# Hybrid decoder layer: a second buffer for the convolution phases, early gate results on ScalarE's queue, the last merged block by halves, first and last stage regrouped

## The chip, the cores and the metric

The kernel runs on one core of one Trainium2 chip. A core has TensorE (PE in the profile), VectorE (DVE), ScalarE (ACT), GpSimd (POOL) and SyncE (SP), which work side by side, each through its own instructions in order, and wait for each other by semaphores. Transfers between DRAM and the on-chip memory are issued by SP, POOL or ACT and carried by 16 DMA engines. The metric is the time of one execution on the device in microseconds (us), as a median over several runs.

## The reference

One layer of a decoder on 1024 tokens of 1024 channels, all in float32. A gated mixer runs a causal depthwise convolution of 31 taps and an attention of 8 heads on the same projected input, merges the two through sigmoid gates, and a SwiGLU block follows.

```python
def hybrid_mixer(h, ...):
    proj = h @ w_in
    glu_in, qkv, gates = jnp.split(proj, [2 * CONV_WIDTH, 2 * CONV_WIDTH + 3 * ATT_WIDTH], axis=-1)
    u_val, u_gate = jnp.split(glu_in, 2, axis=-1)
    u = u_val * jax.nn.sigmoid(u_gate)
    u = causal_depthwise_conv(u, conv_w, conv_b)
    u = jax.nn.silu(layernorm(u, conv_ln_g, conv_ln_b))
    y_conv = u @ w_conv_out
    o = stick_breaking_attention(q, k, v)
    y_att = o.reshape(b, s, ATT_WIDTH) @ w_att_out
    g_conv, g_att = jnp.split(gates, 2, axis=-1)
    merged = jax.nn.sigmoid(g_conv) * y_conv + jax.nn.sigmoid(g_att) * y_att
    return merged @ w_o

def reference(x, c, ...):
    h = rmsnorm(x, pre_mix_g[l]) * (1.0 + sc1) + sh1
    y = hybrid_mixer(h, ...)
    x = x + ga1 * rmsnorm(y, post_mix_g[l])
    h = rmsnorm(x, pre_ffn_g[l]) * (1.0 + sc2) + sh2
    gate, up = jnp.split(h @ w_ffn_in, 2, axis=-1)
    y = (silu(gate) * up) @ w_ffn_out
    return x + ga2 * rmsnorm(y, post_ffn_g[l])
```

## The kernel before, in words

Activations lie with the channels on the 128 partitions and the tokens along the row. A large product keeps float32 accuracy by splitting each operand into a rounded high part (copied by ScalarE) and a low part (the difference, taken by VectorE): each product of two tiles is then three TensorE matmuls, high by high, high by low and low by high. The gate products and the SwiGLU block save one product in eight by a Strassen-like scheme, whose sums and differences VectorE forms. A scheduler places the instructions of each engine before the kernel runs, from the order of the code, priorities and the buffers' free times; once placed, an engine's order is fixed.

The stages that the change touches, in order of time:

- **First stage.** `rstd`, shifts and scales, then for each of the eight channel blocks k the products of three weight blocks (`pq0`, `pk0`, `pgg0`) by `gemm_k`. ScalarE and VectorE are pinned to the order of the code, TensorE isn't.
- **Convolution.** `conv(ct)` runs for four blocks of 128 channels (ct 0 to 3), with the attention heads between. The gated input `u` is stored to `v_d[ct]` and read back transposed into `ph` (L440 to L442), whose first columns POOL sets to zero. Then 40 tile products per block, 20 for each half, go through TensorE (`pcv`, L453; each is two records in the trace) with five weight tiles `cvw`, which rotate through three buffers. Both the stores (`v_d`, `u_d`) and the loads (`ph`, `cvw`) stand in SP's queue, in order. `ph` has one buffer, so the load of `ph` for one block is issued when the products of the block before have read it.
- **Early gate products.** For seven gate pairs i, `early(i, q)` forms two of the seven products of the scheme with q 0 and 1 in one PSUM bank `k` out of three. After each, ScalarE reads the bank into `ee` (L624), one of two buffers `sg` of 256 KB, and the result goes to DRAM (`e_d0`, shown as `e_d`, or `s_d`) by `store`, which is POOL's queue (L101). The next user of a bank waits for its `ee`, and an `ee` waits until the store of the one two before has landed. At the same time SP loads sixteen pieces of the input (`f<-xm_d`, 256 KB each), from which VectorE forms operands (L674 to L677) that ScalarE and VectorE split into `T1o` to `T4o` (L147, L660).
- **Merge.** For each of eight blocks n: two products `pya`, VectorE multiplies by the gate (L840) and adds (L841), and `split_r` splits the 1024 columns of the block into `mhi` (ScalarE) and `mlo` (VectorE). The output product `pwo` (L900) then takes, in its first pass, the first 512 columns of each block.
- **Last stage.** The second product of the SwiGLU block (`ka`, L1524) in sweeps, the norm and the residual. `x_tile` has four buffers, `acc` two and `rs` two.

The profile's line numbers are those of the kernel before. After the change lines from L370 on are 3 higher, and from the merge on 11 higher.

Of the kernel before, what the change touches and what calls it, by code (L numbers as in the profile page):

```python
# [10 lines left out]
F32 = mybir.dt.float32  # L11
F32R = mybir.dt.float32r
AF = mybir.ActivationFunctionType
ALU = mybir.AluOpType
# [3 lines left out]
P = 128  # L18
D = 1024
T = 1024  # L20
KT = D // P
CH = 512
# [47 lines left out]
def tile_block(ctx: ExitStack, tc: tile.TileContext, xT, vecs, ada1, ada2, win, wv, wcv, wat, wo, w1, w2, cvw, out):  # L70
# [29 lines left out]
    def store(dst, src):  # L100
        nc.gpsimd.dma_start(dst, src)  # L101
# [97 lines left out]
    with ExitStack() as s0:  # L199
# [146 lines left out]
        for k in range(KT):  # L346
# [18 lines left out]
            if k <= 1:  # L365
                for i in range(k + 1):
                    gemm_k(ws[i], w0s[i], k)
                for kk in range(k + 1):
                    gemm_k(ws[k + 1], w0s[k + 1], kk)
            else:  # L370
                for b_, w_ in zip(ws, w0s):
                    gemm_k(b_, w_, k)
        high.__exit__(None, None, None)
        pin(begin, START_PIN)
# [32 lines left out]
    with ExitStack() as sC:  # L407
        pc = mkpool(sC, "pc")
        with ExitStack() as sA:
# [28 lines left out]
            def conv(ct):  # L438
                ph = pc.tile([P, NG, SH - 1 + TM], F32, tag="ph", name=f"ph{ct}", bufs=1)
                pool.memset(ph[:, :, 0:SH - 1], 0.0)  # L440
# [174 lines left out]
            def early(i, q):  # L615
# [8 lines left out]
                act.activation(e, k, (AF.Copy, AF.Sigmoid)[q])  # L624
                store(s_d[2 * i][:, :CH] if q else e_d0[i], e)

# [7 lines left out]
    with ExitStack() as sG:  # L634
# [195 lines left out]
        for n in range(KT):  # L830
# [6 lines left out]
            for c in range(NCH):  # L837
# [3 lines left out]
                dve.tensor_tensor(y[:, cs], y[:, cs], sg[c], op=ALU.add)  # L841
            hi, lo = split_r(y, (f"mhi{n}", f"mlo{n}"), act, dve)
            mhi.append(hi)
            mlo.append(lo)
        assert not a2
# [643 lines left out]
    with ExitStack() as sG:  # L1489
# [10 lines left out]
        def x_tile(name):  # L1500
            return px.tile([P, 2, CH], F32, tag="xr", name=name, bufs=4)

# [134 lines left out]
        def sum_sq(name, ys):  # L1637
            acc = pg.tile([P, CH], F32, tag="acc", name=name, bufs=2)
            for n, y in enumerate(ys):
                if n == 0:  # L1640
                    act.activation(acc, y, AF.Square)
                else:
                    sq = sq_tile(f"{name}_{n}")
                    act.activation(sq, y, AF.Square)
                    add(dve, acc, acc, sq)
            return acc

        def finish(c, h, ps_sum, yy, last=None):
            n = ps_sum.shape[-1]
            cols = slice(h * n, (h + 1) * n)  # L1650
            dcols = slice(c * CH + h * n, c * CH + (h + 1) * n)
            rs = pg.tile([P, CH], F32, tag="rs", name=f"frs{c}{h}", bufs=2)[:, :n]
            m, a = (sq_tile(f"frs{c}{h}{i}")[:, :n] for i in "ma")
# [162 lines left out]
```

## Time and profile before

| | us |
|---|---|
| median of 3 runs | 1413.03 (1412.89 to 1413.87) |
| the profiled execution's own time | 1414.92 |
| its span, first to last instruction | 1413.2 |
| ScalarE busy | 655.3 (46%) |
| VectorE busy | 1048.3 (74%) |
| GpSimd busy | 117.4 (8%) |

The mean clock granted to TensorE is 0.990 of full speed. A row of the timeline reads: start in us, duration in us, engine, line, operation, output tile <- input tiles, shapes, how many such instructions stand behind one another (x), and in brackets how long the engine sat idle before it and what ended that. A row of waits reads: engine and line that waited <- what released it, us in total, times, longest. Consecutive matmuls overlap, so the distance of their starts, not their duration, is what one costs.

### The profile page before, as it was taken

What the parts mean: (1) busy time and instruction counts of PE and PEld (TensorE: products, weight loads), DVE (VectorE), ACT (ScalarE), POOL (GpSimd) and SP (SyncE); (2) the same over time, 40 slices, a digit from 0 to 9 for tenths busy, and PEclk for the clock granted to TensorE, in tenths of its full rate; (3) what the DMA queues carried; (4) which work ended last, traced back from release to release, by engine and by line L of the source; (5) the groups of instructions that cost most, each with busy time, mean ns of one, the idle gap of its engine ahead of it and who ended that gap; (6) DMA issues with size and microseconds to landing.
All of it is one profiled execution on the core that took longest, in us unless ns stands there. A gap on an engine that the chain in (4) does not pass through costs nothing.

```text
span 1413.2 us, 18854 instructions
## 1 busy us (share of the span) xinstructions
PE 1378.3 (98%) x6810; PEld 1157.3 (82%) x6810; DVE 1048.3 (74%) x1591; ACT 655.3 (46%) x1146; POOL 117.4 (8%) x262
## 2 busy tenths in 40 slices
PE   7999999999998999999999999999999999999996
PEld 5898898998886788788877778888888887888886
DVE  7897687675865888878589878778877776785355
ACT  6375566364554455512356553334434443434441
POOL 0100001000001111000011110001111110000002
PEclk8999999999999999999999999999999999999998
DMA  9512051140348554973934545456777769586736
GB/s 382 200 39 82 16 164 30 46 150 30 120 150 298 208 170 148 349 226 124 360 120 163 182 148 177 165 171 212 260 250 246 264 240 387 177 337 221 254 116 120
DMA packets 93789, 265.02 MB, mean 188 GB/s; under 512 B 10048, under 2 KB 21440, under 8 KB 92672
## 3 DMA queue, kind: packets, MB, share of 16 engines
q1 hardware_dynamic: 74352, 201.68, 42.0%
q0 software_dynamic: 19344, 62.14, 12.4%
q8 instruction: 53, 0.87, 0.3%
q14 instruction: 40, 0.33, 0.1%
HBM read 192.74 MB, written 71.04 MB: 187 GB/s over the span
## 4 chain that ended last, share of the span: by engine, by line
PE 75%; issue 9%; DVE 8%; DMA 4%; ACT 2%; POOL 1%; SPq 0%; DVEq 0%; POOLq 0%; ACTq 0%
PE ka L982 14%; PE ka L1524 9%; PE kc L982 8%; PE pwo L900 6%; PE pb L1524 4%; PE pgv L168 3%; PE pv L473 3%; PE pgg L168 2%; PE pk L168 2%; PE pq L168 2%; PE ke L1090 2%; PE pcv L453 2%; PE tr L566 2%; PE pa L1524 2%; PE kb L982 2%
## 5 line engine op out<-in xcount | busy, mean ns | idle before, releaser
L545 ACT ACTIVATE ka<-z 128x128 f32<-128x128 f32 (+2 forms) x96 | 47.0, 496 | 55.8 <-PE z L544 51.9
L551 DVE TENSOR_TENSOR_SCAN ka<-ka,eye 128x128 f32<-128x128 f32 (+1 forms) x64 | 52.1, 831 | 23.2 <-ACT ka L545 23.0
L570 DVE TENSOR_TENSOR alo<-tr,ahi 128x512 fp32r<-128x512 f32 x80 | 53.4, 685 | 21.3 <-ACT ahi L569 20.7
L569 ACT ACTIVATE ahi<-tr 128x512 fp32r<-128x512 f32 x80 | 46.7, 603 | 39.1 <-PE av L575 22.9
L1524 PE MATMUL ka<-gt,w2f 128*128 128x512 f32 x264 | 63.4, 389 | 0.0
L556 DVE TENSOR_TENSOR be<-be,ka 128x127 f32<-128x127 f32 (+2 forms) x96 | 51.2, 550 | 12.1 <-ACT be L547 8.5
L1524 PEld LDWEIGHTS ka<-gt,w2f 128*128 128x128 f32 x264 | 49.5, 188 | 10.3
L123 DVE SCALAR_TENSOR_TENSOR ada<-ada,cb 128x1024 f32<-128x1024 f32 x32 | 38.9, 1223 | 23.6 <-DMA ada<-in_ada_dram 23.4
L1090 PE MATMUL ke<-b,w_hi 128*128 128x512 f32 x176 | 55.2, 395 | 0.0
L547 ACT ACTIVATE be<-z 128x127 f32<-128x127 f32 (+2 forms) x96 | 46.4, 496 | 17.8 <-PE tr L566 17.6
L566 PE MATMUL tr<-ident,be 128*128 128x128 f32 x288 | 46.6, 272 | 0.0
L453 PE MATMUL pcv<-ph,cvw 128*128 128x128 f32 x320 | 43.7, 282 | 2.5 <-DMA ph<-v_d 2.5
L554 DVE TENSOR_TENSOR_SCAN ka<-ka 128x512 f32<-128x512 f32 x32 | 40.4, 1274 | 6.3 <-ACT ka L545 6.3
L404 PE MATMUL k<-hhi,a 128*128 128x512 f32 x112 | 38.3, 413 | 6.6 <-ACT ee L624 6.6
L453 PEld LDWEIGHTS pcv<-ph,cvw 128*128 128x128 f32 x320 | 41.5, 198 | 3.5 <-issue 2.7
L575 PE MATMUL av<-ahi,vst 128*128 128x256 f32 x160 | 43.8, 291 | 0.0
L576 PE MATMUL av<-alo,vst 128*128 128x256 f32 x160 | 42.2, 290 | 0.0
L1090 PEld LDWEIGHTS ke<-b,w_hi 128*128 128x128 f32 x176 | 32.9, 188 | 7.9 <-issue 1.0
L147 ACT ACTIVATE gt<-X 128x512 fp32r<-128x512 f32 x33 | 20.3, 629 | 39.4 <-DVE X L1567 14.3
L473 PE MATMUL pv<-wv_hi,hhi 128*128 128x256 f32 x128 | 36.7, 287 | 1.6 <-DVE vst L478 0.9
L147 ACT ACTIVATE s1o<-s 128x512 fp32r<-128x512 f32 x22 | 13.8, 629 | 48.8 <-PE ka L982 41.0
L473 PE MATMUL pv<-wv_lo,hhi 128*128 128x256 f32 x128 | 36.3, 285 | 0.0
(545 smaller groups left out, 4145.8 us busy)
## 6 DMA issues: line engine op xcount, KB each, us to landing
w_d<-w2o POOLq DMA_DIRECT2D x44, 512.0 KB, 7.6
w2f<-w_d SPq DMA_DIRECT2D x44, 512.0 KB, 4.5
ada<-in_ada_dram SPq DMA_DIRECT2D x32, 512.0 KB, 5.7
w2r<-in_w_dram SPq DMA_DIRECT2D x44, 256.0 KB, 3.8
w1g<-in_w_dram SPq DMA_DIRECT2D x21, 512.0 KB, 3.7
w1u<-in_w_dram SPq DMA_DIRECT2D x21, 512.0 KB, 5.7
cvw<-in_cvw_dram SPq DMA_DIRECT2D x20, 512.0 KB, 3.8
ada_w<-in_ada_dram SPq DMA_DIRECT2D x8, 1024.0 KB, 13.9
```

The costliest lines, as they stand in the source:

```text
L168: pe.matmul(bank, st[:, cols], mv[k][:, c * CH:(c + 1) * CH], start=(i == 0 and s == 0), stop=(i == n - 1 and s == 2))
L453: pe.matmul(cv[:, gi * TM:(gi + 1) * TM], wts[n][:, at:at + P], ph[:, g, SH - 1 - d:SH - 1 - d + TM], start=(d == 0), stop=(d == SH - 1))
L473: pe.matmul(pv[:, :256], st[k][:, tcols], mv[:, wc], start=(k == 0 and i == 0), stop=(k == KT - 1 and i == 2))
L545: act.activation(kap[:, s_lo:s_hi], z[:, zo:zo + w], AF.Sigmoid, bias=0.0, scale=-0.125)
L551: dve.tensor_tensor_scan(rev, rev, eye[:, CH - w:][:, ::-1], 0.0, op0=ALU.mult, op1=ALU.add)
L556: dve.tensor_tensor(beta[:, :m], beta[:, :m], kap[:, s_lo + 1:s_lo + 1 + m], op=ALU.mult)
L566: pe.transpose(tr[:, o:o + P], src, ident)
L570: dve.tensor_tensor(alo, tr, ahi, op=ALU.subtract)
L900: pe.matmul(bank_, st[:, cols], mv[k][:, cs], start=(k == 0 and q == 0), stop=(k == KT - 1 and q == 2))
L982: pe.matmul(bank_, st[:, cols], t[:, mv], start=(first and j == 0 and s == 0), stop=(j == HK - 1 and s == 2), skip_group_check=not first)
L1090: pe.matmul(kbs[f], wes[f][st][:, cols], t[:, mv], start=(i == 0 and j == 0 and q == 0), stop=(j == HK - 1 and q == 2), skip_group_check=i ...
L1524: pe.matmul(dst, w[st][:, cols], g[mv], start=first and s == 0, stop=last and s == 2, skip_group_check=more)
```

## The change

The last two channel blocks of the first stage are taken per weight block. `ph` gets a second buffer. The store of `ee` is issued by ScalarE itself, behind the `ee` that it stores. The last merged block is split in two halves of 512 columns, each with its own `mhi` and `mlo` instruction. In the last stage `x_tile` gets a fifth buffer, `rs` a third, and `acc` and `rs` lie in another pool.

```diff
--- before.py
+++ after.py
@@ -367,9 +367,12 @@
                     gemm_k(ws[i], w0s[i], k)
                 for kk in range(k + 1):
                     gemm_k(ws[k + 1], w0s[k + 1], kk)
-            else:
+            elif k < KT - 2:
                 for b_, w_ in zip(ws, w0s):
                     gemm_k(b_, w_, k)
+        for b_, w_ in zip(ws, w0s):
+            for k in (KT - 2, KT - 1):
+                gemm_k(b_, w_, k)
         high.__exit__(None, None, None)
         pin(begin, START_PIN)
         sg0 = []
@@ -436,7 +439,7 @@
                 load(channels(v_d[ct]), u)
 
             def conv(ct):
-                ph = pc.tile([P, NG, SH - 1 + TM], F32, tag="ph", name=f"ph{ct}", bufs=1)
+                ph = pc.tile([P, NG, SH - 1 + TM], F32, tag="ph", name=f"ph{ct}", bufs=2)
                 pool.memset(ph[:, :, 0:SH - 1], 0.0)
                 load(ph[:, :, SH - 1:], v_d[ct].rearrange("g p m -> p g m"))
                 wts = []
@@ -622,7 +625,7 @@
                 prod0(k, w, ("B11", "B21")[q], q == 0)
                 e = sgp.tile([P, CH], F32, tag="sg", name=f"ee{q}_{i}", bufs=2)
                 act.activation(e, k, (AF.Copy, AF.Sigmoid)[q])
-                store(s_d[2 * i][:, :CH] if q else e_d0[i], e)
+                act.dma_start(s_d[2 * i][:, :CH] if q else e_d0[i], e)
 
             for n, i in enumerate(GPAIRS):
                 early(i, 0)
@@ -839,9 +842,17 @@
                 load(sg[c], s_d[8 + n][:, cs])
                 last = dve.tensor_tensor(sg[c], yb[c], sg[c], op=ALU.mult)
                 dve.tensor_tensor(y[:, cs], y[:, cs], sg[c], op=ALU.add)
-            hi, lo = split_r(y, (f"mhi{n}", f"mlo{n}"), act, dve)
-            mhi.append(hi)
-            mlo.append(lo)
+                if n < KT - 1:
+                    continue
+                if c == 0:
+                    mhi.append(hp.tile([P, T], F32R, tag="act", name=f"mhi{n}"))
+                    mlo.append(hp.tile([P, T], F32R, tag="act", name=f"mlo{n}"))
+                act.activation(mhi[n][:, cs], y[:, cs], AF.Copy)
+                dve.tensor_tensor(mlo[n][:, cs], y[:, cs], mhi[n][:, cs], op=ALU.subtract)
+            if n < KT - 1:
+                hi, lo = split_r(y, (f"mhi{n}", f"mlo{n}"), act, dve)
+                mhi.append(hi)
+                mlo.append(lo)
         assert not a2
         add_bias(16, 32)
         fold_gate(gpost1, 16, C_POST1)
@@ -1498,7 +1509,7 @@
             return hp.tile([P, 2, CH], dt, tag="act", name=name)
 
         def x_tile(name):
-            return px.tile([P, 2, CH], F32, tag="xr", name=name, bufs=4)
+            return px.tile([P, 2, CH], F32, tag="xr", name=name, bufs=5)
 
         def bank(name):
             return psg.tile([P, CH], F32, tag="main", name=name)
@@ -1635,7 +1646,7 @@
             return po_.tile([P, CH], F32, tag="wt", name=name, bufs=3)
 
         def sum_sq(name, ys):
-            acc = pg.tile([P, CH], F32, tag="acc", name=name, bufs=2)
+            acc = px.tile([P, CH], F32, tag="acc", name=name, bufs=2)
             for n, y in enumerate(ys):
                 if n == 0:
                     act.activation(acc, y, AF.Square)
@@ -1649,7 +1660,7 @@
             n = ps_sum.shape[-1]
             cols = slice(h * n, (h + 1) * n)
             dcols = slice(c * CH + h * n, c * CH + (h + 1) * n)
-            rs = pg.tile([P, CH], F32, tag="rs", name=f"frs{c}{h}", bufs=2)[:, :n]
+            rs = px.tile([P, CH], F32, tag="rs", name=f"frs{c}{h}", bufs=3)[:, :n]
             m, a = (sq_tile(f"frs{c}{h}{i}")[:, :n] for i in "ma")
             rstd_from(rs, m, a, ps_sum, D)
             for m in range(4):
```

What it moves in the engines' orders is shown at three places; in the names the numbers at the end tell buffers apart.

TensorE at the change from the convolution of block 2 to that of block 3, before, where `pcv_0_4111` is the first half of block 3, `ph_4108` its input, and `z`, `tr`, `av` belong to the attention (`z_1_5_1` head 1, row block 5):

```order
L576 MATMUL av_0_1_3777<-alo_0_1_0_3817,vst_0_2496 128x256
L543 MATMUL z_1_4_1_3950<-kst_1_3035,qst_1_3033 128x256
L544 MATMUL z_1_4_1_3950<-klo_1_3037,qst_1_3033 128x256
L453 MATMUL pcv_0_4111<-ph_4108,cvw_0_4113 128x128 x8
L453 MATMUL pcv_0_4111<-ph_4108,cvw_1_4123 128x128 x3
L543 MATMUL z_1_5_1_3960<-kst_1_3035,qst_1_3033 128x256
L544 MATMUL z_1_5_1_3960<-klo_1_3037,qst_1_3033 128x256
L453 MATMUL pcv_0_4111<-ph_4108,cvw_1_4123 128x128 x2
```

After, from the first product of block 3 on:

```order
L456 MATMUL pcv_0_4111<-ph_4108,cvw_0_4113 128x128
L546 MATMUL z_1_6_0_3907<-kst_1_3035,qst_1_3033 128x512
L547 MATMUL z_1_6_0_3907<-klo_1_3037,qst_1_3033 128x512
L456 MATMUL pcv_0_4111<-ph_4108,cvw_0_4113 128x128
L546 MATMUL z_1_7_0_3915<-kst_1_3035,qst_1_3033 128x512
L547 MATMUL z_1_7_0_3915<-klo_1_3037,qst_1_3033 128x512
L578 MATMUL av_0_1_3777<-ahi_0_1_1_3803,vst_2_2551 128x256
L579 MATMUL av_0_1_3777<-alo_0_1_1_3804,vst_2_2551 128x256
L578 MATMUL av_0_1_3777<-ahi_0_1_1_3803,vst_2_2551 128x256
L579 MATMUL av_0_1_3777<-alo_0_1_1_3804,vst_2_2551 128x256
L578 MATMUL av_0_1_3777<-ahi_0_1_0_3816,vst_0_2496 128x256
L456 MATMUL pcv_0_4111<-ph_4108,cvw_0_4113 128x128 x4
```

Before, all of the products of block 3 stand behind `z_1_4_1`; after, the first stands ahead of `z_1_6_0` and all that follows it, and when `z_1_5_1` comes, twelve instead of eleven of them have been issued. On SP's queue the load of `ph_4108` now stands two transfers behind the store of its `v_d`, ahead of the last weight tile of block 2 and of all weights of block 3.

ScalarE in the early gate products, before, where `ee_2_4434` is the second result of pair 2 and `T2o_4643` to `T4o_4652` are the operands from the third group of `f`:

```order
L147 ACTIVATE T3o_4625<-f_1_4607 128x512
L624 ACTIVATE ee_3_4416<-k_4400 128x512
L147 ACTIVATE T4o_4628<-f_1_4610 128x512
L147 ACTIVATE a_6_4518<-ew_4515 128x512
L147 ACTIVATE a_6_4554<-ew_4515 128x512
L147 ACTIVATE T2o_4643<-f_2_4633 128x512
L147 ACTIVATE T1o_4646<-f_2_4632 128x512
L147 ACTIVATE T3o_4649<-f_2_4631 128x512
L147 ACTIVATE T4o_4652<-f_2_4634 128x512
L624 ACTIVATE ee_2_4434<-k_4361 128x512
```

After:

```order
L147 ACTIVATE T3o_4625<-f_1_4607 128x512
L147 ACTIVATE a_6_4518<-ew_4515 128x512
L147 ACTIVATE a_6_4554<-ew_4515 128x512
L147 ACTIVATE T4o_4628<-f_1_4610 128x512
L147 ACTIVATE T2o_4643<-f_2_4633 128x512
L147 ACTIVATE T1o_4646<-f_2_4632 128x512
L147 ACTIVATE T3o_4649<-f_2_4631 128x512
L627 ACTIVATE ee_2_4434<-k_4361 128x512
L628 DMA s_d_83<-ee_2_4434 128x512
L147 ACTIVATE T4o_4652<-f_2_4634 128x512
```

`ee_2_4434` moves ahead of `T4o_4652`, `ee_3_4416` (shown before only) ahead of `T2o_4619`, and each `ee` is followed by a transfer that ScalarE issues. On VectorE the operation L676 of the third group, `f_2_4633`, now stands directly behind the low part of `T2o_4619`, where before `f_3_4656` and the low parts of `T1o_4622` and `T3o_4625` came between.

TensorE at the first use of the last merged block (`mhi_6159`, `mlo_6160`) in `pwo_0`, before:

```order
L900 MATMUL pwo_1_6227<-mhi_5913,wo_1_hi 128x512
L900 MATMUL pwo_1_6227<-mlo_5914,wo_1_hi 128x512
L900 MATMUL pwo_1_6227<-mhi_5913,wo_1_lo 128x512
L900 MATMUL pwo_0_6192<-mhi_6159,wo_0_hi 128x512
L900 MATMUL pwo_1_6227<-mhi_5957,wo_1_hi 128x512
L900 MATMUL pwo_1_6227<-mlo_5958,wo_1_hi 128x512
L900 MATMUL pwo_1_6227<-mhi_5957,wo_1_lo 128x512
L900 MATMUL pwo_1_6227<-mhi_5995,wo_1_hi 128x512
```

After (there it is called `mhi_6156`, `mlo_6157`):

```order
L911 MATMUL pwo_1_6229<-mhi_5913,wo_1_lo 128x512
L911 MATMUL pwo_1_6229<-mhi_5957,wo_1_hi 128x512
L911 MATMUL pwo_1_6229<-mlo_5958,wo_1_hi 128x512
L911 MATMUL pwo_0_6194<-mhi_6156,wo_0_hi 128x512
L911 MATMUL pwo_1_6229<-mhi_5957,wo_1_lo 128x512
L911 MATMUL pwo_1_6229<-mhi_5995,wo_1_hi 128x512
L911 MATMUL pwo_1_6229<-mlo_5996,wo_1_hi 128x512
L911 MATMUL pwo_0_6194<-mlo_6157,wo_0_hi 128x512
```

Two more products of `pwo_1` stand ahead of it than before. In the last stage the order of all engines is the same up to the names.

## The prediction

> **What bounds the kernel now.** The first view is the page's list of busy times, the second the list of who waited for whom on TensorE.
>
> ```profile
> span 1413.2 us, 18854 instructions
> PE 1378.3 (98%) x6810; PEld 1157.3 (82%) x6810; DVE 1048.3 (74%) x1591; ACT 655.3 (46%) x1146; POOL 117.4 (8%) x262
> ```
>
> ```profile
> PE k L404 <- ACT ee L624: 6.6, 4, 4.0
> PE pcv L453 <- DMA ph<-v_d: 2.5, 1, 2.5
> PE pwo L900 <- ACT mhi L147: 1.3, 1, 1.3
> PE ka L1524 <- ACT gb L147: 1.2, 1, 1.2
> PE pv L473 <- DVE qst L497: 0.8, 1, 0.8
> ```
>
> TensorE is busy for 1378.3 of 1413.2 us, so only 34.9 us of the span can be won without taking work away from it. The change takes no matmul away and adds none. What it can win is therefore in gaps of TensorE and in the slower clock that follows a gap. Three of the rows above are waits that the change aims at: 6.6 us for the results of the early gate products, 2.5 us for the convolution's input, 1.3 us for the last merged block. Together that is 10.4 us. The other two rows stand where the first and the last stage are regrouped.
>
> Whether a gap costs more than its length is read from the granted clock (column after the five busy times, 1.00 is full speed) in stretches around the two longest gaps.
>
> ```profile
> 384.50:388.00 3.50, 3.50 (x18) 3.50 (x19) 1.58 (x4) 0.00 (x0) 0.00 (x0) 0.55 0.25 78
> 450.00:460.00 10.00, 6.04 (x24) 4.35 (x24) 10.00 (x17) 5.67 (x12) 1.08 (x2) 1.00 1.00 382
> 460.00:467.00 7.00, 6.07 (x15) 4.76 (x16) 7.00 (x12) 3.69 (x8) 1.07 (x2) 0.52 0.51 181
> ```
>
> Behind the convolution gap the clock was 0.55 for 3.5 us, and 0.52 in the 7 us that hold the end of the longest early gap and what follows. So both gaps are paid for twice.
>
> The Trainium skill ("TensorE: Matmul & The Clock Gate", Part 1: The HAM clock gate) says that the array falls to half speed after at least one idle window of about 3.4 us. The trace disagrees for the first gap, which was 2.5 us long and was followed by 0.55; by the page's rule the convolution term below would be the gap alone, 2.5 us. The row decides.
>
> **Convolution: second buffer for `ph`.** SP's and TensorE's timelines at the change from block 2 to block 3:
>
> ```profile
> 366.13 0.33 SPq L98 DMA_DIRECT2D v_d<-u  x1
> 377.20 0.33 SPq L98 DMA_DIRECT2D cvw<-in_cvw_dram  x1
> 379.03 0.38 SPq L98 DMA_DIRECT2D ph<-v_d  x1
> 379.50 0.53 SPq L98 DMA_DIRECT2D cvw<-in_cvw_dram  x1
> ```
>
> ```profile
> 376.12 2.84 PE L453 MATMUL pcv<-ph,cvw 128*128 128x128 f32 x24
> 381.68 0.28 PE L544 MATMUL z<-klo,qst 128*128 128x256 f32 x1
> 384.49 4.32 PE L453 MATMUL pcv<-ph,cvw 128*128 128x128 f32 x22 [2.54 <-DMA ph<-v_d]
> 388.57 0.36 PE L543 MATMUL z<-kst,qst 128*128 128x256 f32 x1
> ```
>
> The gated input is stored at 366.13, but its load into `ph` is issued at 379.03, as soon as the last products of block 2 (376.12 plus 2.84 is 378.96) have let go of the one buffer. It takes until 384.5, and TensorE stands for 2.54 us. Then 22 records of `pcv` take 388.57 minus 384.49, or 4.08 us. At full clock 24 of them took 2.84, or 0.118 each, so 22 would take 2.60: the slow clock cost another 1.48. With a second buffer the load waits only for the store to land. A transfer of this size took 5.5 us here (379.03 to 384.49), so even store and load one after the other, issued from 366.13, are over at 377.1, ahead of the first use, which now stands at about 379.2. The weights `cvw` of block 3 are next: their second tile is issued at 377.20, the third at 379.50. With 5.5 us for each they land at 382.7 and 385.0; the new order needs the second at about 383.7 (where the first eight products and `z_1_4_1` are done) and the third two microseconds later. Both fit, by about a microsecond. The gain is 2.54 plus 1.48, **4.0 us**. Bounds: 2.5 if TensorE meets another short wait that keeps the clock down, 4.5 if more of block 3 fits under waits of the attention. SP now waits in order at `ph` for the store's landing, which holds the last weight tile of block 2 behind it until about 370; it is used from about 377 on (the last sixteen of the records at 376.12). The loads for blocks 1 and 2 move ahead in the same way, but TensorE has no wait for `ph` there, so they count nothing.
>
> **Early gate results on ScalarE's queue.** TensorE's gaps and ScalarE's row of work in front of them:
>
> ```profile
> 450.10 0.50 PE L404 MATMUL k<-hhi,a 128*128 128x512 f32 x1 [1.21 <-ACT ee L624]
> 453.91 0.50 PE L404 MATMUL k<-hhi,a 128*128 128x512 f32 x1 [0.79 <-ACT ee L624]
> 460.93 0.80 PE L404 MATMUL k<-hhi,a 128*128 128x512 f32 x1 [4.01 <-ACT ee L624]
> 469.22 2.88 PE L404 MATMUL ka<-T2o,s2o 128*128 128x512 f32 x12
> ```
>
> ```profile
> 442.51 0.60 ACT L624 ACTIVATE ee<-k 128x512 f32<-128x512 f32 x1 [2.80 <-DMA e_d<-ee]
> 449.46 0.58 ACT L624 ACTIVATE ee<-k 128x512 f32<-128x512 f32 x1
> 457.30 0.63 ACT L147 ACTIVATE T2o<-f 128x512 fp32r<-128x512 f32 x1 [1.88 <-DVE f L676]
> 459.77 0.63 ACT L147 ACTIVATE T4o<-f 128x512 fp32r<-128x512 f32 x1 [0.80 <-DVE f L677]
> 460.30 1.07 ACT L624 ACTIVATE ee<-k 128x512 f32<-128x512 f32 x2
> ```
>
> Only the `ee` at 442.51 waited for a store to land. The long gap, 4.01 us, ends with the `ee` at 460.30, which had its buffer and its bank long before; it stands in ScalarE's order behind `T2o` to `T4o` of the third group of `f`, and these wait for VectorE, which is busy 10.00 of 10 us from 450 to 460. So the faster issue of a store wins little by itself; what counts is the order that came with it. There `ee_2` stands ahead of `T4o_2`, and VectorE's L676 of that group comes directly behind the low part of `T2o_1`:
>
> ```profile
> 454.11 0.69 DVE L660 TENSOR_TENSOR T2o<-f,T2o 128x512 fp32r<-128x512 f32 x1
> 456.52 0.75 DVE L676 SCALAR_TENSOR_TENSOR f<-f,mod,f 128x512 f32<-128x512 f32 x1
> ```
>
> L676 then runs from 454.7 to 455.5 instead of from 456.52 to 457.27. ScalarE's `T2o`, `T1o` and `T3o` follow at about 0.53 apart, and `ee_2` starts at 455.5 plus 1.6, or 457.1, instead of 460.30. That is **3.2 us** for TensorE's next product, and this gap shrinks from about 4.0 to 3.5 only, since the two short ones ahead of it (1.21, 0.79) go into it: so I leave the slow clock behind it as it is. Its price is in the rows: 24 products from 460.93 to 469.22 take 8.29 us, and twelve at full speed 2.88 less one overhang of 0.39, over eleven steps, 0.226 each, so 24 would take 5.43 and the penalty is 2.86.
>
> What speaks for less are the transfers that ScalarE now carries. Their price on ScalarE isn't in the trace; the nearest rows are POOL's and SP's issues.
>
> ```profile
> 450.34 0.54 POOL L101 DMA_DIRECT2D s_d<-ee  x1 [5.34 <-ACT ee L624]
> ```
>
> ```profile
> 433.41 11.90 SPq L98 DMA_DIRECT2D f<-xm_d  x14
> ```
>
> ```profile
> f<-xm_d SPq DMA_DIRECT2D x16, 256.0 KB, 6.8
> e_d<-ee POOLq DMA_DIRECT2D x7, 256.0 KB, 5.7
> ```
>
> Alone on SP an issue shows 0.33 (the `v_d` row), POOL's is 0.54, and in the stretch that fills the DMA engines SP needed 11.90 for 14, or 0.85 each. Fourteen stores so cost ScalarE 4.6 to 11.9 us over 45 us in which it is about half busy. I take 0.33, since ScalarE issues one at a time and not fourteen in a row; the four between 442.51 and `ee_2` then cost 1.3 us, which the waits for VectorE (1.88 and others) cover. An issue also waits in the program for an earlier transfer of SP's with which it shares a semaphore. There it could be held for up to one landing, 6.8 us. Bounds of this edit: all gaps and the penalty gone, 6.6 plus 2.86, a gain of 9.5; or a loss, worked out as the last rival below.
>
> The Trainium skill ("DMA: Bandwidth & Descriptors", Issuing engines are not separate DMA queues; "Trainium Kernel Development and Optimization", Key Constraints) says that transfers from SP, ACT and POOL run on the same 16 engines, so that issuing from several saves issue time only. The trace agrees as far as it goes: in the same stretch stores from POOL took 5.7 us and loads from SP 6.8. By this rule alone the term would be near nothing, the first rival.
>
> **Last merged block by halves.**
>
> ```profile
> 669.54 1.29 DVE L841 TENSOR_TENSOR yc<-yc,sga 128x512 f32<-128x512 f32 x2
> 670.87 1.06 ACT L147 ACTIVATE mhi<-yc 128x1024 fp32r<-128x1024 f32 x1 [3.88 <-DVE yc L841]
> 671.97 0.73 PE L900 MATMUL pwo<-mhi,wo_hi 128*128 128x512 f32 x2 [1.27 <-ACT mhi L147]
> ```
>
> The first half of `yc` is ready at 669.54 plus about 0.65, its `mhi` of 512 columns takes 0.63 (the `T2o` row), so it is done at 670.85 instead of 671.95. TensorE fell idle at 670.70 and now has two more products (0.45) to do first. So the gap of 1.27 closes, a gain of **1.2 us** (bounds 0.6, if the second half comes between, and 1.3). The halves cost ScalarE and VectorE one more instruction start each, where ScalarE has been idle for 3.88 us. The low part is needed three products later and comes in time.
>
> **First and last stage.** In the first stage the last products of `pq0` end at the same row of TensorE's order, and the next wait there (0.8, for `qst` out of `pq0`) hangs on these: 0, within half a microsecond. In the last stage the order is the same, only waits for buffers change. The 1.2 us wait is for an operand `gb` that stands behind others on ScalarE, not for a buffer of the pools in question: 0, again within half a microsecond.
>
> **The sum.** 4.0 + 3.2 + 1.2 = 8.4. The profiled execution would go from 1414.92 to 1406.5. It lies 1.89 above the median, so the predicted median is 1413.03 minus 8.4, or **1404.6 us**.
>
> **The rivals.**
> 1. *Only the queue changes, the early gap stays.* VectorE's full 10 us speak for it: an `ee` that comes sooner may only move the wait to the next operand. Against it speaks that the `ee` itself waits for nothing of VectorE's. 1413.03 minus 4.0 and 1.2: 1407.8.
> 2. *The early gap goes far enough that the clock holds.* 3.5 us of rest is still longer than the 2.54 that lost the clock, but if ScalarE gets ahead in the waits before, the whole 9.5 goes: 1413.03 minus 14.7, 1398.3. The Trainium skill ("TensorE: Matmul & The Clock Gate", Part 1: The HAM clock gate) would put such a gap on its threshold of about 3.4 us.
> 3. *The convolution gap stays*, because a weight tile takes the place of `ph`; the margin is about a microsecond. 1413.03 minus 4.4: 1408.6.
> 4. *Slower: ScalarE's queue is held by its own stores.* From 450 to 467 ScalarE is idle for 17 minus 5.67 and 3.69, or 7.6 us. Holds up to that sum cost nothing. Two full holds of 6.8 make 13.6, delay TensorE by 6.0, win nothing in this stage and keep the clock down for another 2.86: 1407.8 plus 8.9, or 1416.7. It decides from about 12.7 us of holds on, where 1415.8 is passed. Against it: the loads with which a store shares its semaphore were mostly issued eight transfers before.
>
> **Chances.** Forecast 0.58, rival 1 0.17, rival 2 0.09, rival 3 0.08, rival 4 0.06, and 0.02 for none. A measurement of this kernel can tell about 0.2%, 2.8 us, from no change: faster is below 1410.2, slower above 1415.9. Forecast and rivals 1 to 3 are faster, but 1 and 3 lie 2.4 and 1.6 us inside the border, and both together would be 1411.8; I give 0.86 to faster, 0.08 to the same, 0.06 to slower. The forecast's own range is 1402.5 to 1406.5; the range that also takes in rivals 1 to 3 and the bounds is 1398.3 to 1409.5.
>
> **What would show it.** In the waits of TensorE the row `pcv` for `ph` is gone, and no row of `pcv` for `cvw` is in its place; the clock around there stays at 1.00. The wait of `k` for `ee` falls from 6.6 to about 3.5, in one gap near 450, followed by a clock near 0.5. The row `pwo` for `mhi` is gone. ScalarE's waits show no transfer that `f` brings in. Wrong would be a wait of 3 us or more of ScalarE in front of an `ee`, or a new wait of `ka` for `s2o` that gives back what `k` wins.

## The result, and the profile after

The median went from 1412.89 us (11 runs) to 1408.77 us (11 runs, 1406.51 to 1412.43). The ratio is 0.9968 with a 95% interval of 0.9956 to 0.9981, by which the gain is 4.5 us (2.7 to 6.2); the medians differ by 4.1. The forecast was 8.4 us and a median of 1404.6, the range 1398.3 to 1409.5. The profiled execution took 1409.45 us. First the busy times and TensorE's waits of the changed kernel, the same two views as before:

```profile
span 1407.7 us, 18838 instructions
PE 1375.9 (98%) x6810; PEld 1154.8 (82%) x6810; DVE 1047.9 (74%) x1592; ACT 656.3 (47%) x1147; POOL 109.5 (8%) x248
```

```profile
PE k L407 <- ACT ee L627: 4.6, 4, 2.8
...
PE ka L407 <- ACT s2o L147: 3.0, 2, 1.7
...
PE ka L1535 <- ACT gb L147: 1.2, 1, 1.2
...
PE pv L476 <- DVE qst L500: 0.8, 1, 0.8
```

The waits of `pcv` for `ph` and of `pwo` for `mhi` are gone. `k` waits for `ee` 2.0 us less than before. A row that was not there stands below it: `ka` now waits 3.0 us for `s2o`, an operand that VectorE and ScalarE form.

The convolution's place, on SP and TensorE:

```profile
366.17 0.33 SPq L98 DMA_DIRECT2D v_d<-u  x1
...
369.32 0.37 SPq L98 DMA_DIRECT2D ph<-v_d  x1
```

```profile
376.14 2.84 PE L456 MATMUL pcv<-ph,cvw 128*128 128x128 f32 x24
...
379.26 0.39 PE L456 MATMUL pcv<-ph,cvw 128*128 128x128 f32 x2
...
384.41 0.36 PE L546 MATMUL z<-kst,qst 128*128 128x256 f32 x1
```

The load of `ph` is issued 3.2 us after its store, not 13, and the first products of block 3 run at 379.26. The last row is the `z_1_5_1` that began at 388.57 before, so TensorE is 4.16 us ahead here. The clock in the stretches of the prediction (the number behind the five busy times):

```profile
384.50:388.00 3.50, 3.50 (x34) 3.50 (x33) 3.36 (x8) 1.82 (x5) 0.20 (x2) 1.00 0.80 200
...
450.00:460.00 10.00, 6.69 (x29) 4.86 (x27) 10.00 (x18) 5.45 (x11) 0.00 (x0) 1.00 1.03 409
460.00:467.00 7.00, 5.80 (x17) 4.31 (x18) 6.81 (x12) 5.33 (x10) 0.00 (x0) 0.76 0.65 217
```

Behind the convolution the clock is 1.00 instead of 0.55. In the early stage VectorE is again busy for the whole of 450 to 460. The waits of TensorE there, and what ScalarE did in front of the longest:

```profile
453.75 0.50 PE L407 MATMUL k<-hhi,a 128*128 128x512 f32 x1 [2.82 <-ACT ee L627]
460.78 0.73 PE L407 MATMUL ka<-T2o,s2o 128*128 128x512 f32 x2 [1.27 <-ACT s2o L147]
461.93 0.50 PE L407 MATMUL k<-hhi,a 128*128 128x512 f32 x1 [0.42 <-ACT ee L627]
...
550.32 0.74 PE L407 MATMUL ka<-T2o,s2o 128*128 128x512 f32 x2 [1.69 <-ACT s2o L147]
```

```profile
452.61 0.61 ACT L147 ACTIVATE T3o<-f 128x512 fp32r<-128x512 f32 x1
453.13 0.57 ACT L627 ACTIVATE ee<-k 128x512 f32<-128x512 f32 x1
453.73 0.33 ACTq L628 DMA_DIRECT2D s_d<-ee  x1
455.23 0.63 ACT L147 ACTIVATE T4o<-f 128x512 fp32r<-128x512 f32 x1 [1.52 <-DVE f L680]
```

`ee_2` runs at 453.13, right behind `T3o`. TensorE was 4.4 us ahead by then: its first early product began at 423.81, before at 428.23. So this is 457.5 on the old clock, where the prediction had 457.1 and the kernel before 460.30, 2.8 us later. The longest wait shrank by less, from 4.01 to 2.82, since TensorE itself now comes to it 1.6 us sooner. And 1.27 us of waiting follow at 460.78 and 1.69 at 550.32, where there was none; a wait of 0.90 for `gv`, at 569.10 before, is gone. The two new waits have their rows on ScalarE and VectorE:

```profile
460.10 0.63 ACT L147 ACTIVATE s2o<-gs 128x512 fp32r<-128x512 f32 x1 [0.57 <-DVE gs L706]
...
543.60 0.68 DVE L706 TENSOR_TENSOR gs<-gs,gw6a 128x512 f32<-128x512 f32 x1
...
546.94 0.63 ACT L787 ACTIVATE hhi<-lm 128x512 fp32r<-128x512 f32 x1 [1.74 <-DVE lm L785]
...
549.66 0.61 ACT L147 ACTIVATE s2o<-gs 128x512 fp32r<-128x512 f32 x1
```

The first `s2o` was waiting for VectorE's `gs`. The second had its `gs` from 544.28 on; it stood in ScalarE's order behind `hhi` and others, which had waited for another result of VectorE, `lm`. So the second wait comes 90 us behind the stretch that the prediction looked at, and from ScalarE's order.

### The profile page after: what moved, and what is told of

Same layout as the page of the kernel before. It is cut to its first block, busy times and chain, and to the rows that moved or that the text cites. A ratio compares the mean times of both kernels' runs of the same rounds, so it can differ in the third digit from the quotient of the medians.

```text
span 1407.7 us, 18838 instructions
## 1 busy us (share of the span) xinstructions
PE 1375.9 (98%) x6810; PEld 1154.8 (82%) x6810; DVE 1047.9 (74%) x1592; ACT 656.3 (47%) x1147; POOL 109.5 (8%) x248
## 4 chain that ended last, share of the span: by engine, by line
PE 84%; DVE 8%; DMA 4%; ACT 2%; issue 2%; SPq 0%; DVEq 0%; ACTq 0%
PE ka L993 13%; PE ka L1535 9%; PE kc L993 7%; PE pwo L911 6%; PE pb L1535 4%; PE pgv L168 3%; PE pyc L739 3%; PE pya L168 3%; PE pv L476 3%; PE tr L569 2%; PE pgg L168 2%; PE pq L168 2%; PE pk L168 2%; PE pcv L456 2%; PE ke L1101 2%; PE pa L1535 2%
```

## The experiments

Kernels whose label begins with b_ are the kernel before with one edit; those with a_ are the changed kernel with one part undone or added. "Before" was run beside each of them, so ratios are compared, not medians.

**Which edit carries the gain.** Each main edit alone, and the changed kernel with the stores back on GpSimd. The edits:

```diff
# b_ph2: before, and only
-                ph = pc.tile([P, NG, SH - 1 + TM], F32, tag="ph", name=f"ph{ct}", bufs=1)
+                ph = pc.tile([P, NG, SH - 1 + TM], F32, tag="ph", name=f"ph{ct}", bufs=2)
# b_act: before, and only
-                store(s_d[2 * i][:, :CH] if q else e_d0[i], e)
+                act.dma_start(s_d[2 * i][:, :CH] if q else e_d0[i], e)
# b_half: before, and only
-            hi, lo = split_r(y, (f"mhi{n}", f"mlo{n}"), act, dve)
-            mhi.append(hi)
-            mlo.append(lo)
+                if n < KT - 1:
+                    continue
+                if c == 0:
+                    mhi.append(hp.tile([P, T], F32R, tag="act", name=f"mhi{n}"))
+                    mlo.append(hp.tile([P, T], F32R, tag="act", name=f"mlo{n}"))
+                act.activation(mhi[n][:, cs], y[:, cs], AF.Copy)
+                dve.tensor_tensor(mlo[n][:, cs], y[:, cs], mhi[n][:, cs], op=ALU.subtract)
+            if n < KT - 1:
+                hi, lo = split_r(y, (f"mhi{n}", f"mlo{n}"), act, dve)
+                mhi.append(hi)
+                mlo.append(lo)
# a_pool: after, and only
-                act.dma_start(s_d[2 * i][:, :CH] if q else e_d0[i], e)
+                store(s_d[2 * i][:, :CH] if q else e_d0[i], e)
```

> The kernel before with only the second buffer for ph. Theory: the buffer alone gives the convolution's part, 2.5 us of wait and the slow clock behind it, so 4.0 to 4.4 us (ratio 0.9969 to 0.9972); TensorE's wait of pcv for ph is gone and the clock between 380 and 400 us is 1.00. Rival: the gain seen in the changed kernel at this place needs the other edits or is taken back later; then the ratio is 0.999 or above.

> The kernel before with only the stores of the early gate results moved to ScalarE. Theory: ee_2 comes earlier by about 3 us, but a new wait of ka for s2o further on gives back most of it, since VectorE is full there: a net gain of 0.5 to 1.0 us (ratio 0.9993 to 0.9996), waits of k for ee 4 to 5 us, of ka for s2o about 3 us. Rival: the gain is kept where nothing else shifts the stage, 3 us or more (ratio 0.998 or below).

> The kernel before with only the halves of the last merged block. Theory: 1.3 to 1.7 us (ratio 0.9988 to 0.9991), the wait of pwo for mhi gone, and no loss after it. Rival: the loss of 1.3 us that the changed kernel shows between 1000 and 1080 us comes from here; then TensorE's lead over the kernel before falls again to about 0.3 us in that stage.

> The changed kernel with the stores of the early gate results back on GpSimd's queue. Theory: the early stage then is that of the kernel before, 0.5 to 1.0 us slower than the changed kernel, so ratio to before 0.9970 to 0.9978 (about 1409 to 1410 us); waits of k for ee 6.6 us, no wait of ka for s2o. Rival: the queue carries a large part of the gain; then the ratio is 0.998 or above.

Measured: b_ph2 0.9976 (0.9961 to 0.9991), b_act 0.9988 (0.9972 to 1.0003), b_half 1.0003 (0.9991 to 1.0016), a_pool 0.9968 (0.9956 to 0.9980). The buffer alone gives 3.4 us, a little less than expected. The halves alone give nothing that shows, where I expected 1.3 to 1.7 us. With the stores back on GpSimd the changed kernel is as fast as with them on ScalarE, 0.9968 both times. b_act lies between; its interval holds 0 as well as 4 us.

Of b_act the waits show what happened to the early gain, of a_pool that the old waits are back:

```profile
PE k L404 <- ACT ee L624: 4.5, 5, 2.0
PE ka L404 <- ACT s2o L147: 2.8, 2, 2.1
```

```profile
PE k L407 <- ACT ee L627: 6.2, 4, 3.4
...
PE ka L407 <- DVE gv L713: 0.9, 1, 0.9
```

With ScalarE's queue (the first view) the waits of `k` and `ka` in the stage of the gate products sum to 7.3 us, with GpSimd's (the second) to 7.1. Over the eleven profiles of kernels that do the same work in this stage, those further down included, the sum is 7.1 to 7.7 in the five with GpSimd's queue and 6.1 to 7.6 in the six with ScalarE's. Up to 470 us the six do wait less, 4.4 to 5.9 us against 6.2 to 6.8. Near 550 each of the six then waits 1.6 to 2.1 us for `s2o`, in the same ScalarE order as above, and the five wait 0.9 for `gv` near 565. Most of what the wait loses at one place it gets back at another.

**Undoing one part.** Then the changed kernel without the halves, with one buffer for `ph`, and without the regrouping of the first and last stage:

```diff
# a_nohalf: after, and the edit of b_half taken back
-                if n < KT - 1:
-                    continue
...
-            if n < KT - 1:
-                hi, lo = split_r(y, (f"mhi{n}", f"mlo{n}"), act, dve)
...
+            hi, lo = split_r(y, (f"mhi{n}", f"mlo{n}"), act, dve)
...
# a_ph1: after, and only
-                ph = pc.tile([P, NG, SH - 1 + TM], F32, tag="ph", name=f"ph{ct}", bufs=2)
+                ph = pc.tile([P, NG, SH - 1 + TM], F32, tag="ph", name=f"ph{ct}", bufs=1)
# a_noreg: after, and
-            elif k < KT - 2:
+            else:
...
-        for b_, w_ in zip(ws, w0s):
-            for k in (KT - 2, KT - 1):
-                gemm_k(b_, w_, k)
...
-            return px.tile([P, 2, CH], F32, tag="xr", name=name, bufs=5)
+            return px.tile([P, 2, CH], F32, tag="xr", name=name, bufs=4)
...
-            acc = px.tile([P, CH], F32, tag="acc", name=name, bufs=2)
+            acc = pg.tile([P, CH], F32, tag="acc", name=name, bufs=2)
...
-            rs = px.tile([P, CH], F32, tag="rs", name=f"frs{c}{h}", bufs=3)[:, :n]
+            rs = pg.tile([P, CH], F32, tag="rs", name=f"frs{c}{h}", bufs=2)[:, :n]
```

> The changed kernel without the halves of the last merged block. Theory: the wait of pwo for mhi came from how the products around it happened to be placed before (the kernel before with only the second ph buffer, and no halves, shows no such wait), so TensorE has no wait there without the halves either, and the time is that of the changed kernel, within 0.5 us (ratio to before 0.9965 to 0.9972). Rival: the halves close the wait; then the wait of 1.3 us is back and the ratio is 0.9975 or above.

> The changed kernel with one buffer for ph again. Theory: the wait of pcv for ph is back with 2 to 2.5 us, and the slow clock behind it in some executions only, so 2 to 4 us slower than the changed kernel (ratio to before 0.9985 to 0.9995). Rival: the other edits alone carry the gain; then the ratio stays at 0.997.

> The changed kernel without the regrouping of the first and the last stage. Theory: both are worth 0, so the time is that of the changed kernel (ratio to before 0.996 to 0.9978), the same waits at 68 and 1180 us. Rival: the regrouped first or last stage carries 1 us or more; then the ratio is 0.998 or above.

Measured: a_nohalf 0.9979 (0.9966 to 0.9992), a_ph1 0.9996 (0.9984 to 1.0009), a_noreg 0.9954 (0.9941 to 0.9966). Without the second buffer the gain is gone: 0.9996 against 0.9968 is 0.28%, or 4.0 us, and `pcv` waits 1.9 us for `ph` again. Without the halves there is no wait of `pwo` for `mhi` either, though the ratio is 1.5 us worse, within the intervals, and outside what I expected. Without the regrouping the kernel isn't slower; 0.9954 is the best ratio of the study and better than I expected, but its interval overlaps that of the changed kernel, so it isn't shown to be faster.

To see the stages without the noise of whole runs, take two waits that every profile has, of `pv` for `qst` in the first stage and of `ke` for `w_lo` in the SwiGLU stage, and between them the first early product, `k`, which stands behind the convolution. Before, after, b_ph2 and a_ph1 (`k` in the first two only):

```profile
67.94 0.35 PE L473 MATMUL pv<-wv_hi,hhi 128*128 128x256 f32 x1 [0.77 <-DVE qst L497]
...
428.23 0.39 PE L404 MATMUL k<-hhi,a 128*128 128x512 f32 x1
...
800.25 0.50 PE L1090 MATMUL ke<-b,w_lo 128*128 128x512 f32 x1 [0.84 <-DVE w_lo L1024]
```

```profile
67.60 0.36 PE L476 MATMUL pv<-wv_hi,hhi 128*128 128x256 f32 x1 [0.77 <-DVE qst L500]
...
423.81 0.39 PE L407 MATMUL k<-hhi,a 128*128 128x512 f32 x1
...
793.40 0.50 PE L1101 MATMUL ke<-b,w_lo 128*128 128x512 f32 x1 [0.84 <-DVE w_lo L1035]
```

```profile
67.61 0.36 PE L473 MATMUL pv<-wv_hi,hhi 128*128 128x256 f32 x1 [0.77 <-DVE qst L497]
...
791.55 0.50 PE L1090 MATMUL ke<-b,w_lo 128*128 128x512 f32 x1 [0.80 <-DVE w_lo L1024]
```

```profile
67.68 0.36 PE L476 MATMUL pv<-wv_hi,hhi 128*128 128x256 f32 x1 [0.77 <-DVE qst L500]
...
796.09 0.50 PE L1101 MATMUL ke<-b,w_lo 128*128 128x512 f32 x1 [0.84 <-DVE w_lo L1035]
```

From the first wait to the second: 732.3 us before, 725.8 after, 723.9 with only the second buffer, 728.4 with all but the second buffer. The same distances read from the other profiles, with the wait of `pcv` for `ph` where it exists and whether half clock followed it; those of before2, after2 and a_t34pool come further down, and the two kernels with extra matmuls are left out:

| kernel | second buffer | wait for `ph`, us (half clock behind it) | 68 to the first `k`, us | 68 to 800, us | ratio to before |
|---|---|---|---|---|---|
| before | no | 2.5 (yes) | 360.3 | 732.3 | |
| before2 | no | 1.5 (no) | 357.7 | 726.9 | |
| b_half | no | 2.3 (no) | 359.0 | 729.8 | 1.0003 |
| b_act | no | 1.9 (yes) | 360.2 | 728.3 | 0.9988 |
| a_ph1 | no | 1.9 (yes) | 359.8 | 728.4 | 0.9996 |
| after | yes | | 356.2 | 725.8 | 0.9968 |
| after2 | yes | | 356.7 | 724.4 | |
| b_ph2 | yes | | 356.2 | 723.9 | 0.9976 |
| a_pool | yes | | 356.3 | 725.1 | 0.9968 |
| a_nohalf | yes | | 356.3 | 724.2 | 0.9979 |
| a_noreg | yes | | 356.3 | 724.2 | 0.9954 |
| a_t34pool | yes | | 356.5 | 730.0 | 1.0017 |

Up to the first `k` the two groups are far apart, whatever the queue, the halves and the regrouping: 357.7 to 360.3 without the second buffer, 356.2 to 356.7 with it. The means, 359.4 and 356.3 without a_t34pool, differ by 3.1 us, and each kernel with one buffer lies above the others by about its wait and the slow clock behind it. Whether half clock follows isn't set by the length of the wait alone, as two rows show, of b_act and of b_half:

```profile
384.35 4.29 PE L453 MATMUL pcv<-ph,cvw 128*128 128x128 f32 x22 [1.94 <-DMA ph<-v_d]
```

```profile
384.14 2.69 PE L453 MATMUL pcv<-ph,cvw 128*128 128x128 f32 x22 [2.28 <-DMA ph<-v_d]
```

The same 22 records take 4.29 us behind the shorter wait and 2.69 behind the longer one. Over the whole distance to 800 the groups differ too, 729.1 and 724.6 in the mean, and don't overlap if a_t34pool, which changes VectorE's work behind the first `k`, is left out. From the first `k` to 800 the five with GpSimd's queue take 367.8 to 372.0 us and the six with ScalarE's 367.8 to 369.6; the means are 1.4 us apart, but a gain of the queue isn't shown by ranges that overlap so far.

**The same programs once more.** The kernel before and the changed kernel were profiled a second time.

> The kernel before, unchanged, profiled once more. Theory: the waits of TensorE are the same within 0.5 us each (pcv for ph 2 to 2.5, k for ee 6 to 7), but whether the slow clock follows a wait differs from execution to execution, so the clock behind at least one of the waits at 384 and 461 us can be 1.00 here, and the time lies by up to 4 us off the 1414.9 of the first profile. Rival: the clock follows the length of the wait; then both stretches show 0.5 again.

> The changed kernel, profiled once more. Theory: no wait of pcv; waits of k for ee and ka for s2o together 6.5 to 7.7 us; where the slow clock falls between 450 and 470 us, and the small waits of ka for uw between 1000 and 1100 us (1.1 us in the first profile), differ from the first profile, so the time lies within 4 us of 1409.5. Rival: both come again as they were, and belong to the change.

The executions took 1413.31 and 1411.35 us. In after2 the waits of `k` and `ka` sum to 6.1 us, a little under what I expected. Of before2, TensorE's waits for `ph` and `mhi`, and the clock around the first:

```profile
PE pcv L453 <- DMA ph<-v_d: 1.5, 1, 1.5
...
PE pwo L900 <- ACT mhi L147: 0.2, 1, 0.2
```

```profile
386.00:388.00 2.00, 0.48 (x5) 0.44 (x5) 1.87 (x4) 1.34 (x4) 0.00 (x0) 1.00 1.06 365
388.00:390.00 2.00, 2.00 (x20) 2.00 (x19) 2.00 (x5) 0.00 (x0) 0.00 (x0) 1.00 0.49 149
```

In this execution of the same program the wait for `ph` was 1.5 us instead of 2.5, no slow clock followed, and `pwo` waited 0.2 us instead of 1.3. So two of the costs that the prediction read off one profile were not there in another. What made up for it is the start: the wait of `pv` for `qst` came at 72.03 us in before2 and at 67.94 in before. The same happened between after and after2, here in windows of both:

```profile
26.00:33.00 7.00, 7.00 (x27) 6.14 (x26) 6.96 (x9) 2.46 (x4) 0.58 (x2) 0.54 1.00 414
33.00:41.00 8.00, 8.00 (x48) 7.02 (x49) 7.93 (x11) 2.35 (x3) 1.05 (x2) 1.00 1.02 423
```

```profile
26.00:33.00 7.00, 7.00 (x24) 6.13 (x25) 6.96 (x9) 2.42 (x4) 0.57 (x1) 0.50 1.02 424
33.00:41.00 8.00, 8.00 (x28) 6.94 (x28) 7.93 (x11) 2.38 (x3) 1.07 (x2) 0.50 1.01 415
```

In both, TensorE runs at half clock from about 22 us. In the one it ends by 33, in the other at 41, though TensorE is busy throughout from 26 us on. In the second it gets through 28 instead of 48 matmul records between 33 and 41, and the wait of `pv` comes at 71.59 instead of 67.60. These 4.0 us are nearly as large as the gain of the whole change.

**Taking work off VectorE.** If VectorE's full load sets the waits of the early stage, less of it should shorten them.

```diff
# a_t34pool: after, and
-                B0[b, j] = make_t(f"{b}o_{j}", src, act, dve)
+                B0[b, j] = make_t(f"{b}o_{j}", src, act, pool if b in ("T3", "T4") else dve)
```

> The changed kernel with the low parts of T3o and T4o formed by GpSimd instead of VectorE (eight subtractions, 8 x 0.60 = 4.8 us off VectorE between 440 and 470 us). Theory: in the early stage VectorE's full load sets the waits, and moving the stores only moves them from k to ka; then with VectorE relieved the waits of k for ee and of ka for s2o together fall from 7.6 us to under 4, and the time falls by 2 to 4 us against the changed kernel (ratio to before 0.994 to 0.9955). Rival: ScalarE's order or the transfers set them; then they stay at 7 us or more and the time is that of the changed kernel.

Measured: 1.0017 (1.0003 to 1.0031), 6.9 us worse than the changed kernel by the ratios. VectorE's rows of this kernel show why; the third column from the left is the engine, the second the duration:

```profile
443.56 0.69 DVE L394 TENSOR_TENSOR a<-ew,a 128x512 fp32r<-128x512 f32 x1
444.16 1.78 DVE L663 TENSOR_TENSOR T2o<-f,T2o 128x512 fp32r<-128x512 f32 x1
445.86 1.77 DVE L663 TENSOR_TENSOR T1o<-f,T1o 128x512 fp32r<-128x512 f32 x1
...
453.10 1.75 DVE L663 TENSOR_TENSOR T2o<-f,T2o 128x512 fp32r<-128x512 f32 x1
454.78 0.68 DVE L663 TENSOR_TENSOR T1o<-f,T1o 128x512 fp32r<-128x512 f32 x1
```

```profile
444.05 1.34 POOL L663 TENSOR_TENSOR T3o<-f,T3o 128x512 fp32r<-128x512 f32 x1 [17.64 <-ACT T3o L147]
445.35 1.73 POOL L663 TENSOR_TENSOR T4o<-f,T4o 128x512 fp32r<-128x512 f32 x1
```

A subtraction on VectorE takes 0.69 us, and 1.75 to 1.78 beside one on GpSimd. The eight that moved saved VectorE 4.8 us and cost it 1.07 for each of its own that ran beside them. The scheduler also put `ee_2` behind `T4o` again. The longest wait of `k` grew from 2.82 to 6.04 us, and the waits of `k` and of `ka` for `s2o` from 7.6 to 9.4, where I expected under 4. So the run didn't relieve VectorE, it slowed it, and the wait followed. That speaks for VectorE as what sets the wait, but the changed order of `ee_2` could have done it too, so it isn't shown by this run.

**Filling the wait.** Three extra matmuls, whose result nobody reads, in the wait for `ee_2`, and then two more at the start:

```diff
# a_warm5: after, and behind the second product of pair 3, ahead of the first of pair 5
...
+                    wt = psv.tile([P, CH], F32, tag="av", name="warm5")
...
+                    for _ in range(3):
+                        m_ = pe.matmul(wt, ones, cb[:, :CH], start=True, stop=True).ins
+                        tc.add_manual_dep(m_, prev.name, SCHED)
...
+            tc.add_manual_dep(before5[0], warm5[0].name, SCHED)
# a_warm05: a_warm5, and in the middle of shift_pe(0) and shift_pe(1)
+        fillb = q0b[0]
...
+            return pe.matmul(fillb, ones, cb[:, :CH], start=True, stop=True).ins
...
+                if k < 2 and kt == KT // 2:
+                    got.append(fill())
...
```

> The changed kernel with three extra matmuls of 128x512 (ones by a tile that is there, into a bank that nothing reads; 0.86 us each at full clock, 2.6 us in all) in TensorE's order ahead of the product that waits for ee_2. Theory: the wait of 2.8 to 3.1 us itself cannot be used, but the slow clock that follows it in some executions comes from TensorE standing idle; filled, the clock between 445 and 475 us is 1.00 in every profile, TensorE's wait at this place falls under 0.6 us, and the time is 0 to 1.5 us below the changed kernel (ratio to before 0.9955 to 0.9970). Rival: the slow clock there comes from elsewhere (the short waits after it, or a fixed pattern); then it stays near 0.5 for 2 us or more and the time is that of the changed kernel or up to 0.5 us more.

> As the run before, and two more such matmuls at the start, each in the middle of a group of eight products of 128x1 (the first two groups, about 18 to 23 us), where every profile shows a clock of 0.5 from about 22 to 33 us. Theory: the products of one column leave TensorE nearly idle as the clock sees it; with full matmuls between them the slow stretch shortens, and since TensorE is what runs behind there, the time falls by 2 to 4 us more (ratio to before 0.993 to 0.9955). Rival: VectorE and ScalarE set the pace of the first 40 us; then the clock improves but the time gains less than 1 us, or loses the 1.7 us that the extra matmuls cost.

Measured: a_warm5 0.9963 (0.9950 to 0.9977), a_warm05 0.9990 (0.9974 to 1.0005). In a_warm5 TensorE works where it waited:

```profile
454.56 2.73 PE L636 MATMUL warm<-cb,ones 128*128 128x512 f32 x6
457.82 0.50 PE L407 MATMUL k<-hhi,a 128*128 128x512 f32 x1 [0.53 <-ACT ee L641]
```

The clock is 1.00 from 455 to 468 us, as expected. But a_noreg and b_ph2, which fill nothing, also kept it there, and the time is that of the changed kernel within its interval. Whether filling helps stays open; if it does, by less than can be measured here. At the start the theory fell: with the two matmuls the clock fell at about 24 us, as it did without them in a_pool (21 to 24 over the other profiles), and it stayed down until 41. The ratio is worse than that of a_warm5, though the intervals still touch.

## Why the prediction was right, and which steps of it failed

The direction and the main place of the gain were right: TensorE is busy for 98% of the span in both kernels, and the second buffer for `ph`, which takes away a wait of TensorE, is what wins. The size was about half of the forecast.

- **Convolution, 4.0 us.** Right. The wait went and nothing took its place: by the profile TensorE was 4.16 us ahead, by the runs the buffer is worth 3.4 us alone and 4.0 us on top of the rest. The margins of the weight tiles, given as about a microsecond, held: TensorE shows no wait for `cvw`. The 4.0 was one draw, though, and the dearest: among the five profiles with one buffer the wait was 1.5 to 2.5 us, half clock followed it in three and not in two, and the whole cost was 1.4 to 4.0 us, 3.1 in the mean. The slow clock itself was priced a little low, at 1.48: at full clock the 22 records take 2.44 (b_half), so of the 4.08 about 1.6 were lost. Rival 3 didn't happen.
- **Early gate results, 3.2 us.** Wrong, and this is the term that failed. The step up to "`ee_2` starts at 455.5 plus 1.6, or 457.1, instead of 460.30" came true (457.5). What failed is the sentence after it, "That is 3.2 us for TensorE's next product": it was taken as a gain of the whole stage. TensorE got ahead, and then waited for `s2o` instead, 1.27 us at 460.78, where VectorE's `gs` came last, and 1.69 at 550.32, where `s2o` stood in ScalarE's order. The sum of waits didn't shrink (6.6 plus 0.9, or 7.5, before; 4.6 plus 3.0, or 7.6, after), and the runs show no gain of the queue (0.9968 with it and without it in the changed kernel, each known to about 1.8 us; 1.7 us in b_act, with 0 inside the interval). A gain of about a microsecond isn't excluded; one of 3.2 doesn't fit the two kernels with the second buffer. The prediction named this very wait as what would make it wrong, and gave rival 1 for VectorE; it should have followed the producers of TensorE's operands through the whole of the gate products. Its figure for the remaining gap, 3.5, doesn't come out of the parts it names: 4.01 less 3.2, plus 1.21 and 0.79, is 2.8. That 2.82 was measured is luck, since only one of the two short waits went into the long one.
- **The rivals' sums.** Rival 3's 1408.6 is the nearest to the 1408.77 measured, and that is luck, since its wait was gone. Rival 1's 1407.8 is 1.0 us off, with the mechanism that comes nearest to what the runs show.
- **Last merged block, 1.2 us.** The edit does what it says, but the wait it removes was 1.3 us in one execution and 0.2 in the next of the same program, and it isn't there at all in b_ph2, b_act and a_nohalf, which split the last block whole as well. With the halves it is there once, 0.7 us in a_t34pool. b_half alone shows no gain. a_nohalf puts 1.5 us on the halves, which is within the intervals, so the runs don't settle it. Why `pwo` waited in one execution and not in the other stays open.
- **First and last stage, 0.** Right within the measurement.
- **Rival 4**, the held queue, didn't come: ScalarE's own issues took 0.33 us each, as taken. Four of the fourteen came 0.7 to 2.4 us behind the end of their `ee`, which may be such holds; only one of these, 1.1 us, falls between 450 and 467, where the prediction gave 7.6 us as free. No `ee` waited longer than 2.2 us for a transfer; in after2 the longest such wait was 3.0, which is the border that the prediction set, and in the kernel before it was 2.8.

After the merge the first profile of the changed kernel lost 1.2 us again, between the wait at 793 and that of `ka` for `gb` at 1180 (386.4 against 385.2 us). In after2 it was 0.5, in a_noreg and b_ph2 0. It belongs to the execution and not to the change.

## What to carry to other kernels

A single profile gives one draw of what follows a wait: before a term is made of a slow clock or of a wait of a microsecond, see whether a second profile of the same program has it too. A wait that a reordering shortens is won only if the next operands come sooner too; where VectorE is busy 10 of 10 us, follow it and ScalarE through the rest of the stage and count every wait, also those 90 us later. A second buffer in front of a load that could have been issued 13 us earlier is the safer kind of change: here it took away the cause of the wait, and no new one came.

## What the runs showed of the hardware

- Waits of TensorE for `ph` of 1.5 to 2.5 us were followed by half clock in three executions and not in two, and full clock was lost behind a wait of 1.94 us (b_act) and kept behind one of 2.28 (b_half). The Trainium skill ("TensorE: Matmul & The Clock Gate", Part 1: The HAM clock gate) says that the activity window is free-running and that what follows from it varies from run to run; that agrees. Its threshold of about 3.4 us of idle time doesn't: the trace shows the loss after 1.94.
- The slow stretch at the start ended at 33 us in one execution (after) and at 41 in another of the same program (after2), and the whole run was later by 4.0 us up to the next common wait. That this makes a good part of the scatter of 4 to 8 us among the runs of one kernel is likely but not shown, since only one execution in each was profiled.
- VectorE's subtraction of 128x512 went from 0.69 to 1.75 us beside one on GpSimd. The Trainium skill ("GPSIMD Engine Reference", 1. Specifications) says that the two share their access to the on-chip memory, with contention when VectorE reads two inputs from it. The trace agrees, and the price here was 1.07 us per instruction.
- The median time from issue to landing of the fourteen 256 KB stores of `ee` was 5.5 to 6.3 us in the six profiles with ScalarE's queue and 4.9 to 5.3 in the five with GpSimd's, single ones taking 2.0 to 8.0. So the landing was not faster from ScalarE. Why it was slower isn't shown.
